# A decoder layer with product-key experts: who makes the low part of the score tiles while the gates are built

## The chip, the cores and the metric

The kernel runs on one core of a Trainium2 chip. The metric is the device time of one execution in microseconds. TensorE (PE) multiplies, VectorE (DVE), ScalarE (ACT) and GpSimd (POOL) compute elementwise, SyncE (SP) issues most of the DMAs. Each engine works through a queue of its own in order, and waits on semaphores for the others.

## What is computed

One hybrid decoder layer over 512 tokens of 1024 features. The first part (a gated DeltaNet mixer beside pooling groups) isn't touched. The second part is the expert mixer:

```python
q = (xb @ w_query).reshape(t, PEER_HEADS, 2, PEER_HALF)
scores = jnp.einsum("thpc,hpkc->thpk", q, sk)
s1, i1 = lax.top_k(scores[:, :, 0], PEER_TOPK)
s2, i2 = lax.top_k(scores[:, :, 1], PEER_TOPK)
...
top_s, top_pos = lax.top_k(cand, PEER_TOPK)
gate = jax.nn.softmax(top_s, axis=-1)
u, v = expert_down[idx], expert_up[idx]
act = jax.nn.gelu(jnp.einsum("td,thkd->thk", xb, u))
return jnp.einsum("thk,thkd->td", (gate * act), v)
```

There are 128 x 128 experts, 8 heads and 16 picks of each head. For 384 of the 512 tokens the kernel works densely: it computes gelu of all 16384 scores, multiplies them by a gate matrix that is zero where nothing was picked, and multiplies the result by expert_up. For the other 128 tokens (NG = 1 block) it gathers the picked rows.

## The kernel before

**Tiles.** The 16384 experts are 128 tiles of 128. A score tile is 8 chunks (c = 0 to 7) of three matmuls each: every float32 operand is split into a high part and a low part, and a chunk is w_hi by xn_hi, w_hi by xn_lo and w_lo by xn_hi (mm3, L126 to L128). A tile's weights come by one DMA of 512 KB into w_raw (L607), ScalarE rounds them to w_hi (L612) and another engine subtracts, w_lo = w_raw - w_hi (L613). w_raw, w_hi and w_lo have two buffers each, so the load of tile n + 2 waits until tile n's low part has been made, and its w_hi until tile n's last matmul with w_hi.

**Stages.** (1) The mixer. (2) Queries and top-16 of the dense tokens, with the first 17 ahead tiles. (3) The gates: the tokens go in 96 groups of four. For a group two sets of one-hot rows are made, oa over the first key and ob over the second, one of them scaled by the gate, and four products g_ps = ob by oa (L857) give the group's gate matrix. In seven groups of ten VectorE makes both (four instructions on L850 and one on L852); in three of ten (A_ACT) it makes ob in one instruction (L841) and ScalarE makes oa in eight (L845, L846). ScalarE copies g_ps into stg (L860); after every eighth group GpSimd copies a part of stg to gsb (L866) and SP writes the rest to memory (gmat, L867). stg has one buffer, oa and ob have four, g_ps has six. (4) The accumulation: per expert tile the gates by the scores, split again, by expert_up into acc (L941), with the scores of the 82 remaining tiles computed, and the 26 stored ones fetched, between, and the gathers of the 128 other tokens on GpSimd and VectorE.

**Ahead tiles in the gates.** 46 score tiles (20 in a run and 26 far ones that go to memory as h_far) are computed ahead of the accumulation, 29 of them by the generator ahead_steps, one chunk at a step. Its steps are taken between the groups (take, 20 before the first group and then 2.2 to a group on average). While tile n runs, at its first step (k = 0), tile n + 1 is loaded and split by load_pair(..., nc.gpsimd). VectorE also works off the picks of the gathered tokens there (pick_gathered, 28 pieces, top-16 by MAX8, FIND_INDEX8 and MATCH_REPLACE8, then L686 to L721), each pinned behind the last one-hot instruction of the group, called one.

**Order.** A scheduler orders each engine's queue; tc.issue_after(x) pins what is traced in its block behind x on x's engine. TensorE's order is pinned throughout this stage by pe_last.

Of the kernel before, what the change touches and what calls it, by code (L numbers as in the profile page):

```python
# [7 lines left out]
F32 = mybir.dt.float32  # L8
# [36 lines left out]
AHEAD = RUN + FAR  # L45
LEAD = 4
FAR_TILES = [RUN + ((2 * k + 1) * (NK - RUN)) // (2 * FAR) for k in range(FAR)]
A_ACT = (1, 4, 7)

C_ID, C_U, C_M0, C_MS, C_IO, C_ONE = 0, 128, 256, 384, 384 + 7 * 128, 384 + 8 * 128  # L50
# [22 lines left out]
def hymba_peer_block(ctx, tc, consts, x, nmix, w_in, w_ba, conv_w, a_log, dt_bias, dn_w, w_pool, pool_scale,  # L73
                     w_out, nffn, w_q, sub_k, downT, down, up, nfin, out):
    nc = tc.nc
# [526 lines left out]

    behind = []

    def load_pair(src, eng):
        raw = wp.tile([P, DC, P], F32, name="w_raw", tag="w_raw")
        nc.sync.dma_start(out=raw, in_=src)  # L607
        hi = wp.tile([P, DC, P], F32R, name="w_hi", tag="w_hi")
        lo = wp.tile([P, DC, P], F32R, name="w_lo", tag="w_lo")
        before = behind.pop(0) if behind else None  # L610
        with tc.issue_after(before) if before is not None else ExitStack():
            nc.scalar.activation(hi, raw, AF.Copy)  # L612
        eng.tensor_sub(lo, raw, hi.bitcast(F32))  # L613
        return hi, lo

    def h_slot(i):
        h_tiles[i] = hp[i % (RUN + 1) >= RA].tile([P, TD], F32, name="h_act")
        return h_tiles[i]


    def s_steps(i, pair):
        hi, lo = pair
        ps = ps_s.tile([P, 512], F32, name="s_ps")[:, :TD]
        for c in range(DC):
            s_last[0] = mm3(ps, (hi[:, c, :], lo[:, c, :]), (xn_hi[:, c, NG * P:], xn_lo[:, c, NG * P:]), c == 0,
                            c == DC - 1)
            if c < DC - 1:
                yield
        if i in FAR_TILES:
            ht = hq.tile([P, TD], F32, name="h_far")  # L630
            s_act[0] = nc.scalar.activation(ht, ps, AF.Gelu)
            nc.sync.dma_start(out=hfar[FAR_TILES.index(i)], in_=ht)
        else:
            s_act[0] = nc.scalar.activation(h_slot(i), ps, AF.Gelu)
        yield
# [3 lines left out]
    def s_tile(i, eng):  # L639
        for _ in s_steps(i, load_pair(downT[i], eng)):  # L640
            pass


    ahead = list(range(RUN)) + FAR_TILES
    made = [0]
# [4 lines left out]
            made[0] += 1  # L650


    def ahead_steps():
        pair = load_pair(downT[ahead[made[0]]], nc.gpsimd)
        while made[0] < AHEAD:
            i, now = ahead[made[0]], pair
            made[0] += 1
            for k, _ in enumerate(s_steps(i, now)):
                if not k and made[0] < AHEAD:
                    pair = load_pair(downT[ahead[made[0]]], nc.gpsimd)  # L660
                yield


    def refill(i):
        if i in FAR_TILES:
            nc.sync.dma_start(out=h_slot(i), in_=hfar[FAR_TILES.index(i)])
        else:
            s_tile(i, nc.vector)
# [55 lines left out]
    def softmax(pool, dst, sc, behind=None):  # L724
        n = sc.shape[1]
        nc.vector.tensor_sub(dst, sc, sc[:, :, 0:1].broadcast_to([P, n, K]))
        with tc.issue_after(behind.ins) if behind is not None else ExitStack():
            nc.scalar.activation(dst, dst, AF.Exp)
        sm = pool.tile([P, n], F32, name="sm", bufs=1)
        nc.vector.tensor_reduce(sm, dst, axis=AX.X, op=ALU.add)  # L730
        nc.vector.reciprocal(sm, sm)
        nc.vector.tensor_tensor(dst, dst, sm[:, :, None].broadcast_to([P, n, K]), op=ALU.mult)

    with ExitStack() as fy:
# [45 lines left out]


        steps = ahead_steps()
        taken = 0
        pe_last = s_last[0]

        def take(goal):
            nonlocal taken, pe_last
            while taken < goal:
                with tc.issue_after(pe_last.ins):
                    next(steps, None)  # L790
                pe_last = s_last[0]
                taken += 1
# [15 lines left out]
    with ExitStack() as fy:  # L808
        hq = fy.enter_context(tc.tile_pool(name="hq", bufs=2))
        t0p = fy.enter_context(tc.tile_pool(name="t0p", bufs=1))  # L810


        def pick_gathered():
            for b in range(NG):
                ts0 = t0p.tile([P, PH, K], F32, name="ts0")
                i10 = t0p.tile([P, PH, K], F32, name="i10")
                i20 = t0p.tile([P, PH, K], F32, name="i20")
                for h in range(0, PH, 2):
                    yield from topk(t0p, sc0[:, b, h:h + 2], 2, ts0[:, h:h + 2], i10[:, h:h + 2], i20[:, h:h + 2])
                softmax(t0p, gat[b], ts0)  # L820
                nc.vector.scalar_tensor_tensor(eidx[b], i10.rearrange("p h k -> p (h k)"), 128.0,
                                               i20.rearrange("p h k -> p (h k)"), op0=ALU.mult, op1=ALU.add)

        picks, picked = pick_gathered(), 0
        n_picks = NG * PH // 2 * 7
        gs = fy.enter_context(tc.tile_pool(name="gs", bufs=3))
        p_g = fy.enter_context(tc.tile_pool(name="p_g", bufs=6, space=PSUM))
        gsb0 = gp.tile([P, NTG, GN * TG], F32, name="gsb")
        n_steps = (AHEAD - S_QUERY - S_WAIT) * DC
        take(S_FIRST)  # L830
        ng = 0
        for tg in range(NTG):
            stg = gs.tile([P, NK, TG], F32, name="stg", bufs=1)
            for q in range(TG // 4):
                oa = gs.tile([P, 4, P], F32, name="oa", bufs=4)
                ob = gs.tile([P, 4, P], F32, name="ob", bufs=4)
                ps = p_g.tile([P, 512], F32, name="g_ps")
                t0 = tg * TG + q * 4
                q4 = [P, 4, P]
                if ng % 10 in A_ACT:  # L840
                    one = nc.vector.tensor_tensor(ob, iota[:, None, :].broadcast_to(q4),  # L841
                                            i2t[:, t0:t0 + 4, None].broadcast_to(q4), op=ALU.is_equal)
                    for u in range(4):
                        t = t0 + u
                        nc.scalar.activation(oa[:, u], iota, AF.Abs, bias=n1t[:, t:t + 1])  # L845
                        nc.scalar.activation(oa[:, u], oa[:, u], AF.Relu, scale=ngt[:, t:t + 1], bias=gtt[:, t:t + 1])  # L846
                else:
                    for u in range(4):
                        t = t0 + u
                        nc.vector.tensor_scalar(ob[:, u], iota, i2t[:, t:t + 1], gtt[:, t:t + 1], op0=ALU.is_equal,  # L850
                                                op1=ALU.mult)
                    one = nc.vector.tensor_tensor(oa, iota[:, None, :].broadcast_to(q4),  # L852
                                            i1t[:, t0:t0 + 4, None].broadcast_to(q4), op=ALU.is_equal)
                ng += 1
                with tc.issue_after(pe_last.ins):
                    for u in range(4):
                        pe_last = nc.tensor.matmul(ps[:, u * P:(u + 1) * P], ob[:, u], oa[:, u], start=(u == 0),  # L857
                                                   stop=(u == 3))
                take(S_FIRST + ng * (n_steps - S_FIRST) // (TD // 4))
                nc.scalar.copy(stg[:, :, q * 4:q * 4 + 4], ps.rearrange("p (t i) -> p i t", i=NK))  # L860
                if ng * n_picks // (TD // 4) > picked:
                    with tc.issue_after(one.ins):
                        next(picks)
                    picked += 1
            sv = stg.rearrange("p i t -> p (i t)")
            nc.gpsimd.tensor_copy(gsb0[:, tg, :], sv[:, :GN * TG])  # L866
            nc.sync.dma_start(out=gmat[tg, :, GN * TG:], in_=sv[:, GN * TG:])  # L867

        for _ in picks:
            pass  # L870

    with ExitStack() as fz:
# [73 lines left out]
        for i in range(NK):  # L946
# [3 lines left out]
            raw = up_p.tile([P, D], F32, name="u_raw", bufs=3)  # L950
# [97 lines left out]
```

## Time and profile before

| | |
|---|---|
| median of three runs | 1597.91 us (1595.98 to 1601.22) |
| the profiled execution | 1597.25 us |
| its span, first to last instruction | 1595.5 us |
| TensorE matmul busy | 1543.3 us, 97% |
| VectorE busy | 1291.3 us, 81% |
| ScalarE busy | 692.1 us, 43% |
| GpSimd busy | 556.9 us, 35% |
| GpSimd's w_lo on L613 | 60 instructions, 153.8 us |
| mean granted TensorE clock | 0.994 |

Busy shares are averages over stages with different limits, so the stage of the gates (483 to 711 us) is to be read by itself. Busy time includes time in which an instruction has begun and doesn't get on. Instructions on VectorE overlap by some 0.08 us where they follow each other, so the cost of one is best read from start to start.

### The profile page before, as it was taken

The page shows a single profiled execution, that of the slowest core. Times are in us where ns is not written, and L with a number is a line of the kernel's source. Part 1 is how long each engine was busy: PE and PEld are TensorE (multiplying, and loading weights), DVE is VectorE, ACT ScalarE, POOL GpSimd, SP SyncE. Part 2 cuts the span into 40 slices and gives each one's busy share as a digit, 9 for nine tenths or more (in the row PEclk, how much of TensorE's full clock was granted, in tenths as well). Part 3 has the DMA queues.
Part 4 walks back from the last instruction along what each step waited for, and adds up shares of the span by engine and source line. Part 5 has one row for each costly group of instructions (what it writes and reads, how often), then busy time and mean ns, then how long its engine had stood idle before and what let it go on. Part 6 is the DMA issues. An engine that isn't in the chain of part 4 may idle for free.

```text
span 1595.5 us, 23368 instructions
## 1 busy us (share of the span) xinstructions
PE 1543.3 (97%) x8417; PEld 1391.5 (87%) x8417; DVE 1291.3 (81%) x2652; ACT 692.1 (43%) x1175; POOL 556.9 (35%) x362
## 2 busy tenths in 40 slices
PE   6999999999999899899999999999999999999996
PEld 5889798888899899889888888889989888888885
DVE  5577666699999999996887777778888787888885
ACT  5545343333338687673333333333333333333333
POOL 1000000144464333224454445444444444444331
PEclk9999999999999999999999999999999999999998
DMA  6221221422344455459999999999999999899971
GB/s 210 80 67 55 65 83 41 172 89 85 93 128 149 175 194 220 153 207 387 364 337 327 339 315 317 329 329 334 311 332 311 335 319 334 309 326 340 321 265 61
DMA packets 142388, 367.32 MB, mean 230 GB/s; under 512 B 11232, under 2 KB 65520, under 8 KB 140608
## 3 DMA queue, kind: packets, MB, share of 16 engines
q1 hardware_dynamic: 104416, 228.09, 41.4%
q0 software_dynamic: 37712, 136.69, 23.9%
q8 instruction: 66, 1.08, 0.3%
q10 hardware_dynamic: 144, 1.05, 0.2%
q14 instruction: 50, 0.41, 0.1%
HBM read 331.58 MB, written 34.21 MB: 229 GB/s over the span
## 4 chain that ended last, share of the span: by engine, by line
PE 80%; DVE 17%; ACT 1%; DMA 1%; issue 1%; POOL 1%; SPq 0%; ACTq 0%; DVEq 0%; POOLq 0%
PE acc L941 33%; PE s_ps L126 9%; PE s_ps L128 9%; PE s_ps L127 9%; DVE ob L850 7%; PE pj L127 3%; PE pj L126 3%; PE pj L128 3%; DVE oa L852 3%; PE q_ps L127 2%; PE q_ps L128 2%; PE q_ps L126 2%; PE ups L432 1%; PE p L441 1%; DVE ob L841 1%; PE sc_ps L762 1%
## 5 line engine op out<-in xcount | busy, mean ns | idle before, releaser
L126 PE MATMUL s_ps<-xn_hi,w_hi 128*128 128x384 f32 x1024 | 356.8, 348 | 0.0
L128 PE MATMUL s_ps<-xn_hi,w_lo 128*128 128x384 f32 x1024 | 346.4, 338 | 2.5 <-DVE w_lo L613 1.9
L127 PE MATMUL s_ps<-xn_lo,w_hi 128*128 128x384 f32 x1024 | 345.7, 338 | 0.0
L612 ACT ACTIVATE w_hi<-w_raw 128x1024 fp32r<-128x1024 f32 x144 | 152.9, 1062 | 331.7 <-PE s_ps L127 260.4
L916 POOL DMA_INDIRECT row<-in_down_dram,eidx x128 | 190.0, 1485 | 224.8 <-DVE row L918 194.4
L925 POOL DMA_INDIRECT row<-in_up_dram,eidx x128 | 187.0, 1461 | 222.8 <-DVE xr L927 201.0
L613 POOL TENSOR_TENSOR w_lo<-w_raw,w_hi 128x1024 fp32r<-128x1024 f32 x60 | 153.8, 2564 | 291.1 <-ACT w_hi L612 257.2
L941 PE MATMUL acc<-u_hi,whi 128*128 128x512 f32 x768 | 238.6, 391 | 0.6 <-ACT whi L120 0.6
L941 PE MATMUL acc<-u_lo,whi 128*128 128x512 f32 x768 | 237.6, 389 | 0.0
L941 PE MATMUL acc<-u_hi,wlo 128*128 128x512 f32 x768 | 237.5, 389 | 0.0
L120 ACT ACTIVATE whi<-w 128x384 fp32r<-128x384 f32 x128 | 67.2, 525 | 307.5 <-issue 277.2
L128 PEld LDWEIGHTS s_ps<-xn_hi,w_lo 128*128 128x128 f32 x1024 | 192.9, 188 | 3.5 <-DVE w_lo L613 2.3
L127 PEld LDWEIGHTS s_ps<-xn_lo,w_hi 128*128 128x128 f32 x1024 | 193.2, 189 | 3.2
L126 PEld LDWEIGHTS s_ps<-xn_hi,w_hi 128*128 128x128 f32 x1024 | 193.2, 189 | 3.2
L121 DVE TENSOR_TENSOR wlo<-w,whi 128x384 fp32r<-128x384 f32 x128 | 71.2, 556 | 133.8 <-ACT whi L120 133.6
L927 DVE SCALAR_TENSOR_TENSOR xr<-row,dots,xr 128x1024 f32<-128x1024 f32 x128 | 164.2, 1282 | 9.6 <-DMA row<-in_up_dram,eidx 7.7
L941 PEld LDWEIGHTS acc<-u_lo,whi 128*128 128x128 f32 x768 | 144.3, 188 | 31.3 <-DVE u_lo L121 0.3
L941 PEld LDWEIGHTS acc<-u_hi,wlo 128*128 128x128 f32 x768 | 144.2, 188 | 29.9
L918 DVE SCALAR_TENSOR_TENSOR row<-row,xg 128x1024 f32<-128x1024 f32 x128 | 152.1, 1220 | 15.0 <-DMA row<-in_down_dram,eidx 11.4
L941 PEld LDWEIGHTS acc<-u_hi,whi 128*128 128x128 f32 x768 | 143.0, 188 | 24.4 <-ACT whi L120 0.8
L121 DVE TENSOR_TENSOR u_lo<-u_raw,u_hi 128x1024 fp32r<-128x1024 f32 x128 | 156.0, 1219 | 4.1 <-ACT u_hi L120 4.1
L120 ACT ACTIVATE u_hi<-u_raw 128x1024 fp32r<-128x1024 f32 x128 | 134.3, 1049 | 5.5 <-DMA u_raw<-in_up_dram 2.8
(298 smaller groups left out, 2448.8 us busy)
## 6 DMA issues: line engine op xcount, KB each, us to landing
u_raw<-in_up_dram SPq DMA_DIRECT2D x128, 512.0 KB, 6.2
w_raw<-in_downT_dram SPq DMA_DIRECT2D x128, 512.0 KB, 5.7
gmat<-stg SPq DMA_DIRECT2D x12, 1984.0 KB, 8.4
gsb<-gmat SPq DMA_DIRECT2D x31, 768.0 KB, 7.3
w_raw<-in_w_in_dram SPq DMA_DIRECT2D x20, 512.0 KB, 3.6
w_raw<-in_w_q_dram SPq DMA_DIRECT2D x16, 512.0 KB, 3.6
hfar<-h_far SPq DMA_DIRECT2D x26, 192.0 KB, 2.0
h_act<-hfar SPq DMA_DIRECT2D x26, 192.0 KB, 5.9
```

What stands on the lines that cost most here:

```text
L120: nc.scalar.activation(hi, src, AF.Copy)
L121: nc.vector.tensor_sub(lo, src, hi.bitcast(F32))
L126: nc.tensor.matmul(ps, ahi, bhi, start=first, stop=False)
L127: nc.tensor.matmul(ps, ahi, blo, start=False, stop=False)
L128: return nc.tensor.matmul(ps, alo, bhi, start=False, stop=last)
L612: nc.scalar.activation(hi, raw, AF.Copy)
L613: eng.tensor_sub(lo, raw, hi.bitcast(F32))
L916: nc.gpsimd.indirect_dma_start(out=r, out_offset=None, in_=down, in_offset=bass.IndirectOffsetOnAxis(ap=eidx[b][:, s:s + 1], axis=0))
L918: nc.vector.scalar_tensor_tensor(r, r, 1.0, xg, op0=ALU.mult, op1=ALU.mult, accum_out=dots[:, s:s + 1])
L925: nc.gpsimd.indirect_dma_start(out=r, out_offset=None, in_=up, in_offset=bass.IndirectOffsetOnAxis(ap=eidx[b][:, s:s + 1], axis=0))
L927: nc.vector.scalar_tensor_tensor(xr[b], r, dots[:, s:s + 1], xr[b], op0=ALU.mult, op1=ALU.add)
L941: nc.tensor.matmul(acc[b][n], l[:, bs], r[:, n * 512:(n + 1) * 512], start=(i == 0 and l is whi and r is uhi), stop=(i == NK - 1 and l is ...
```

## The change

The split is taken apart. load_hi starts the DMA and ScalarE's w_hi as before, at the first step of the tile before. The subtraction is traced later, at that tile's fifth step (k = LO_STEP = 4), goes to VectorE, and is pinned behind dve_one, the one of the newest group. The generator's first load uses VectorE as well. make_ahead and the queries keep GpSimd; in the gates GpSimd is left with its 12 copies.

```diff
+LO_STEP = 4
...
-    def load_pair(src, eng):
+    dve_one = [None]
+
+    def load_hi(src):
         raw = wp.tile([P, DC, P], F32, name="w_raw", tag="w_raw")
         nc.sync.dma_start(out=raw, in_=src)
...
             nc.scalar.activation(hi, raw, AF.Copy)
+        return raw, hi, lo
+
+    def load_pair(src, eng):
+        raw, hi, lo = load_hi(src)
         eng.tensor_sub(lo, raw, hi.bitcast(F32))
         return hi, lo
...
     def ahead_steps():
-        pair = load_pair(downT[ahead[made[0]]], nc.gpsimd)
+        pair = load_pair(downT[ahead[made[0]]], nc.vector)
...
                 if not k and made[0] < AHEAD:
-                    pair = load_pair(downT[ahead[made[0]]], nc.gpsimd)
+                    raw, hi, lo = load_hi(downT[ahead[made[0]]])
+                    pair = (hi, lo)
+                if k == LO_STEP and made[0] < AHEAD:
+                    with tc.issue_after(dve_one[0]) if dve_one[0] is not None else ExitStack():
+                        nc.vector.tensor_sub(lo, raw, hi.bitcast(F32))
                 yield
...
                 ng += 1
+                dve_one[0] = one.ins
```

VectorE's queue at the groups 7 to 10 (counted from 0), before: group 7 is one of ScalarE's (ob alone, L841), 8, 9 and 10 are VectorE's own, and MAX and MAX_INDEX are a piece of the picks.

```order
L841 TENSOR_TENSOR ob<-cst,i2t 128x512
L675 MAX val<-rep 128x8
L676 MAX_INDEX idx<-val,rep 128x8
L850 TENSOR_SCALAR ob<-cst,i2t,gtt 128x128 x4
L852 TENSOR_TENSOR oa<-cst,i1t 128x512
L850 TENSOR_SCALAR ob<-cst,i2t,gtt 128x128 x4
L852 TENSOR_TENSOR oa<-cst,i1t 128x512
L850 TENSOR_SCALAR ob<-cst,i2t,gtt 128x128 x4
L852 TENSOR_TENSOR oa<-cst,i1t 128x512
```

The same place of VectorE's queue in the changed kernel, from group 8 on; its lines are 12 or 13 further on, and L672 is the moved subtraction, here that of tile 22.

```order
L862 TENSOR_SCALAR ob<-cst,i2t,gtt 128x128
L687 MAX val<-rep 128x8
L862 TENSOR_SCALAR ob<-cst,i2t,gtt 128x128
L688 MAX_INDEX idx<-val,rep 128x8
L862 TENSOR_SCALAR ob<-cst,i2t,gtt 128x128 x2
L864 TENSOR_TENSOR oa<-cst,i1t 128x512
L862 TENSOR_SCALAR ob<-cst,i2t,gtt 128x128 x4
L864 TENSOR_TENSOR oa<-cst,i1t 128x512
L672 TENSOR_TENSOR w_lo<-w_raw,w_hi 128x1024
L862 TENSOR_SCALAR ob<-cst,i2t,gtt 128x128 x4
L864 TENSOR_TENSOR oa<-cst,i1t 128x512
```

The subtraction of tile 22 now stands between the rows of the tenth and the eleventh group; in TensorE's queue tile 22's chunks begin after the tenth group's products. The picks are interleaved with the rows one by one.

GpSimd's queue from the mixer's last multiplications into the gates, before (the alternation of subtractions and copies goes on to the twelfth copy).

```order
L477 TENSOR_TENSOR tts<-tt,nfp 128x512 x3
L613 TENSOR_TENSOR w_lo<-w_raw,w_hi 128x1024 x37
L866 COPY gsb<-stg 128x128
L613 TENSOR_TENSOR w_lo<-w_raw,w_hi 128x1024 x2
L866 COPY gsb<-stg 128x128
L613 TENSOR_TENSOR w_lo<-w_raw,w_hi 128x1024 x2
L866 COPY gsb<-stg 128x128
```

GpSimd's queue from the same place in the changed kernel, on to the gathers.

```order
L478 TENSOR_TENSOR tts<-tt,nfp 128x512 x3
L620 TENSOR_TENSOR w_lo<-w_raw,w_hi 128x1024 x31
L879 COPY gsb<-stg 128x128 x12
L929 DMA row<-in_down_dram,eidx_2703 128x1024 x128
L938 DMA row<-in_up_dram,eidx_2703 128x1024 x128
```

29 of GpSimd's 60 subtractions are gone, and its 12 copies follow each other. On SP's queue the write of stg stands behind the load of the same tile as before in ten of the twelve places (the first behind that of tile 24), and one load earlier in the other two; each load waits for the low part of the tile two before it. At the end of the stage TensorE's queue has 28 score matmuls ahead of the first accumulation, and had 12.

## Rows read from the trace of the kernel before

**Rows 1.** The page, chain that ended last: shares of the span by line

```profile
PE acc L941 33%; PE s_ps L126 9%; PE s_ps L128 9%; PE s_ps L127 9%; DVE ob L850 7%; PE pj L127 3%; PE pj L126 3%; PE pj L128 3%; DVE oa L852 3%; PE q_ps L127 2%; PE q_ps L128 2%; PE q_ps L126 2%; PE ups L432 1%; PE p L441 1%; DVE ob L841 1%; PE sc_ps L762 1%
```

**Rows 2.** Windows, last stage: length, busy PE, PEld, DVE, ACT, POOL, clock, DMA

```profile
711.30:1540.00 828.70, 826.84 (x4073) 741.37 (x4074) 666.38 (x831) 295.63 (x404) 377.08 (x256) 1.00 0.93 329
```

**Rows 3.** The same view, four stretches of the gates

```profile
483.10:547.50 64.40, 58.28 (x399) 56.49 (x397) 63.78 (x163) 50.86 (x115) 25.43 (x12) 1.00 0.50 179
547.50:600.90 53.40, 51.45 (x351) 50.87 (x351) 52.71 (x156) 39.73 (x92) 15.99 (x9) 0.97 0.47 164
600.90:657.80 56.90, 48.84 (x339) 47.02 (x337) 56.42 (x151) 40.88 (x95) 19.80 (x10) 1.00 0.60 227
657.80:703.60 45.80, 45.14 (x306) 44.65 (x306) 45.59 (x133) 33.05 (x77) 14.19 (x7) 0.96 0.53 186
```

**Rows 4.** Timeline at long VectorE instructions: start, length, engine, line, what

```profile
494.35 2.88 POOL L613 TENSOR_TENSOR w_lo<-w_raw,w_hi 128x1024 fp32r<-128x1024 f32 x1 [3.00 <-ACT w_hi L612]
...
494.90 3.18 DVE L850 TENSOR_SCALAR ob<-cst,i2t,gtt 128x128 f32<-128x128 f32 x4
...
647.27 2.39 DVE L704 TENSOR_SCALAR ta<-pos 128x32 uint32<-128x32 uint32 x1
...
652.29 2.87 DVE L717 TENSOR_TENSOR oh<-oh,idf 128x1024 bf16<-128x1024 bf16 x1
```

**Rows 5.** VectorE's groups, 483.1 to 711.3: busy us, mean ns | idle before

```profile
L850 DVE TENSOR_SCALAR ob<-cst,i2t,gtt 128x128 f32<-128x128 f32 x268 | 117.4, 489 | 0.0
...
L704 DVE TENSOR_SCALAR ta<-pos 128x32 uint32<-128x32 uint32 x4 | 2.9, 726 | 0.0
```

**Rows 6.** Tiles ob, oa, idf, oh: ns min/median/max, first and last start

```profile
L850 DVE TENSOR_SCALAR ob<-cst,i2t,gtt x268: 320/336/2433, 483.7 to 705.0; 128x128 f32<-128x128 f32 x134
...
L852 DVE TENSOR_TENSOR oa<-cst,i1t x67: 662/679/691, 483.1 to 705.3; 128x512 f32<-128x512 f32 x67
...
L686 DVE CAST idf<-idx x4: 184/313/2399, 523.8 to 690.9; 128x64 bf16<-128x64 uint32 x4
...
L717 DVE TENSOR_TENSOR oh<-oh,idf x4: 685/690/2870, 543.3 to 708.6; 128x1024 bf16<-128x1024 bf16 x4
```

**Rows 7.** L850 by groups in the four stretches, in their order

```profile
L850 DVE TENSOR_SCALAR ob<-cst,i2t,gtt 128x128 f32<-128x128 f32 x73 | 37.1, 564 | 0.0
...
L850 DVE TENSOR_SCALAR ob<-cst,i2t,gtt 128x128 f32<-128x128 f32 x69 | 27.3, 449 | 0.0
...
L850 DVE TENSOR_SCALAR ob<-cst,i2t,gtt 128x128 f32<-128x128 f32 x65 | 28.0, 477 | 0.0
...
L850 DVE TENSOR_SCALAR ob<-cst,i2t,gtt 128x128 f32<-128x128 f32 x60 | 24.9, 459 | 0.0
```

**Rows 8.** GpSimd's groups, 483.1 to 711.3

```profile
L613 POOL TENSOR_TENSOR w_lo<-w_raw,w_hi 128x1024 fp32r<-128x1024 f32 x27 | 70.3, 2605 | 131.6 <-ACT w_hi L612 124.7 <-PE g_ps L857 6.9
L866 POOL COPY gsb<-stg 128x128 f32<-128x128 f32 x12 | 5.7, 473 | 21.7 <-ACT stg L860 21.7
```

**Rows 9.** Timeline, a subtraction on VectorE and the instruction behind it

```profile
711.30 1.22 DVE L613 TENSOR_TENSOR w_lo<-w_raw,w_hi 128x1024 fp32r<-128x1024 f32 x1
712.44 1.02 DVE L958 TENSOR_TENSOR w<-h_act,gsb 128x384 f32<-128x384 f32 x2
```

**Rows 10.** Chain in order of time: last rows of the 10th and 78th group

```profile
506.63 0.60 DVE oa L852
...
664.51 0.60 DVE ob L841
```

**Rows 11.** GpSimd's timeline: the low parts of tiles 22 and 41

```profile
501.71 2.38 POOL L613 TENSOR_TENSOR w_lo<-w_raw,w_hi 128x1024 fp32r<-128x1024 f32 x1 [4.48 <-ACT w_hi L612]
...
666.03 2.96 POOL L613 TENSOR_TENSOR w_lo<-w_raw,w_hi 128x1024 fp32r<-128x1024 f32 x1 [10.71 <-ACT w_hi L612]
```

**Rows 12.** Waits, 483.1 to 711.3: us in total, times, longest

```profile
SPq L607 <- POOL w_lo L613: 65.3, 23, 5.5
...
ACT stg L860 <- DMA gmat<-stg: 9.5, 6, 2.5
```

## Prediction

> **What bounds the kernel now.** I read the chain of waits first, then busy time by stretches, then VectorE's groups and the timeline around its longest instructions. The chain lies on TensorE for most of the span, but 11% of it stands on three lines of one-hot rows, L850, L852 and L841, all VectorE [rows 1]. They belong to one stage, 483.1 to 711.3 us: the gates, 96 groups of one-hot rows and products, with the ahead tiles' score chunks between them. Behind it TensorE is the bound: 826.84 of 828.70 us busy [rows 2]. So whatever the gates stage gives or loses goes through to the end unless the start of the last stage changes.
>
> I cut the stage where TensorE had just waited for rows. VectorE is busy 98.8, 98.7, 99.2 and 99.5% of the four stretches; TensorE sits idle 6.1, 2.0, 8.1 and 0.7 us in them [rows 3]. VectorE sets the first and the third; in the second and fourth both engines are nearly full. The last 8 us of the stage hold no subtraction.
>
> VectorE's 99% isn't all work. While GpSimd makes a low part, four instructions on L850 take 3.18 us; a shift (L704) and a product (L717) met the same way took 2.39 and 2.87 [rows 4]. Over the stage L850 averages 489 ns [rows 5] where its median is 336 [rows 6].
>
> **The change part by part.** *GpSimd's subtractions go* (29, of which 27 in this stage). VectorE's stalls behind them: L850, 268 x (489 - 336) = 41.0 us [rows 5, 6]. L704's four take 2.90 in all, the long one 2.39 [rows 4, 5], so the others 0.17: 2.2 us. L717 2870 - 690 = 2.2; L686 2399 - 313 = 2.1 [rows 6]. Together 47.5. By stretch L850 gives 73 x 228 = 16.6, 69 x 113 = 7.8, 65 x 141 = 9.2 and 60 x 123 = 7.4 us [rows 7]; the long L704 and L717 lie in the third, the long L686 (the last of its four, at 690.9) in the fourth: 16.6, 7.8, 13.6, 9.5. I put all of it down to the subtractions: the 12 copies are a fifth as long [rows 8], and stay. If the stalls that touch a copy and no subtraction stay, it is under 1 us.
>
> *VectorE makes them instead.* From one subtraction's start to the next instruction's start is 712.44 - 711.30 = 1.14 us [rows 9]. The stretches hold 9, 6, 7 and 5 of them (GpSimd's counts of 12, 9, 10 and 7 [rows 3] less three, three, three and two copies): 10.3, 6.8, 8.0, 5.7 us, 30.8 in all. VectorE's work so changes by -6.3, -1.0, -5.6 and -3.8, which is -16.7 us.
>
> *What of it reaches the end.* TensorE can't go below its own work, so a stretch gains at most its idle time: min(6.3, 6.1) + min(1.0, 2.0) + min(5.6, 8.1) + min(3.8, 0.7) = 6.1 + 1.0 + 5.6 + 0.7 = 13.4 us.
>
> *The first two unpinned subtractions* (tiles 17 and 18) stand where VectorE waits for transposes and for the exponential; I take 0, at most 2 x 1.14. Tile 19's stands ahead of the first one-hot row and is among the 27.
>
> *The new wait.* A subtraction on VectorE waits for ScalarE's w_hi, with the next group's rows and picks queued behind it, and TensorE waits for those. The order puts tile 22's behind the tenth group's rows. In the trace those rows end at 506.63 + 0.60 = 507.23, and its w_hi had been there at 501.7, when GpSimd began: 5.5 us of slack. The tightest I found is tile 41, behind the 78th group: rows done at 665.11, w_hi at 666.0, a wait of 0.9 [rows 10, 11]. That is a stretch where VectorE was well ahead of TensorE, so the wait takes from a lead. I take 0; the bound is 27 x 0.9 = 24 us.
>
> *The deadline.* TensorE needs the low part for the third matmul of the tile. The order puts the subtraction just after the rows of the last group ahead of the tile, so 1.14 us runs beside that group's eight products and two matmuls. I take 0; in three tiles (24, 26, 37) it stands one group later, where TensorE may wait some 1.4 us but finds the next rows ready: 0 to 4.
>
> *The queues.* SP's load into the freed w_raw slot now waits for a subtraction that comes some 5 us later, and behind four of these loads (before the copies of groups 8, 16, 80 and 88) stands the write of stg, whose slot ScalarE's next copy waits for. SP already waited 65.3 us for low parts, ScalarE 9.5 for that write, 2.5 at most [rows 12]. ScalarE's own rows for three groups in ten are queued behind such a copy. Bounds: 0, and 4 x 2.5 = 10; I take 2, since ScalarE has lead there.
>
> *Start of the last stage.* 16 score matmuls move ahead of the first accumulation, under the wait for the first weights: 0 to -0.6 us; I take 0.
>
> Sum: -13.4 + 2 = -11.4. The profiled execution took 1597.25 us (span 1595.5 and 1.75 around it), 0.66 below the median of the runs shown: 1597.25 - 11.4 = 1585.9, so 1586.
>
> **A rule against it.** L852 has two SBUF inputs, like the subtraction, and its 67 executions stay between 662 and 691 ns although GpSimd subtracts for 70 us of the stage [rows 6, 8]; the product L717, with two inputs as well, was held once. The Trainium skill (SBUF — State Buffer, Who interferes with whom) says that a VectorE instruction with two SBUF inputs contends with a GpSimd instruction that reads SBUF; by that rule, which the L852 row doesn't bear out, the moved subtractions could still wait for the copies, at most 12 x 0.47 = 5.7 us, an estimate, and the sum would be 1591.6.
>
> **The rivals.** *VectorE's whole saving comes through* (TensorE's idle time was only where I cut): 16.7 us, and the granted clock, on average 0.97 and 0.96 of the 2.4 GHz level in the second and fourth stretch [rows 3], comes back whole, 0.03 x 53.4 + 0.04 x 45.8 = 3.4 us: 1577 to 1581. Against it: TensorE is full in the fourth stretch.
>
> *Lead is capped, queues cost more.* Where VectorE is ahead it now waits for w_hi and can't store the lead that the picks' heavy ends use up; with the queues' 5 us half the gain goes: 1590 to 1593.
>
> *The in-order wait takes the gain's place.* If ScalarE's w_hi comes late because ScalarE stands before a stg write, each subtraction holds VectorE. The point: 16.7 / 27 = 0.6 us each cancels the saving. At 0.4 to 0.7 the time is within 0.3%. At 1.0 it is 27 - 16.7 = 10 us slower, 1607. For it: tile 41's 0.9; against: 5.5 us of slack at tile 22, and a wait that comes only with a lead.
>
> *It doesn't do what it says*: the pin only bounds the place from above, and the order shows the subtraction far behind the pinned row, at the tile's edge rather than in mid-tile. That changes the deadline, not VectorE's work, so it has no time and no chance of its own.
>
> **How the numbers follow.** Forecast, 1581 to 1590: 0.55. Whole saving: 0.10. Capped: 0.13. Cancelled, within 0.3%: 0.15. Slower: 0.07. What a measurement of this kernel can tell is about 0.3%, 4.8 us, so faster is below 1593.1: 0.78; same 0.15; slower 0.07. The range 1580 to 1596 leaves out half of the whole saving and the upper part of the last two cases, under 0.2 together.
>
> **What the changed profile would show.** L850's mean falls from 489 to some 340 ns with no instruction over 1 us; VectorE has 27 more subtractions of 1.22 us in the stage; the stage shrinks from 228 to some 216 us, and the rest keeps its length. Wrong would be: VectorE idle before its subtractions, released by ScalarE's w_hi, by more than 5 us; TensorE idle on ScalarE's rows by more than the before; or L850 still stretched.

## The result, and the profile of the changed kernel

The changed kernel took 1575.1 us (median of four runs) against 1597.35 for the kernel before on the same chip: a ratio of 0.9849, 95% interval 0.9837 to 0.9862. That is 22 us faster, twice the 11.4 forecast and 5 us below the low end of the range. The direction was right, the size was not. The profiled execution took 1572.2 us (span 1570.4); it started the changed stage 3.7 us earlier than the profiled execution of before, 2.8 of that in work that neither kernel changes. The first score matmul of the runs below lies anywhere from 323.0 to 327.0 us, whatever the kernel. So I compare lengths inside the trace, and medians.

The page of the changed kernel, chain that ended last, by engine and by line (11% on one-hot rows in [rows 1]):

```profile
PE 92%; DVE 3%; ACT 2%; DMA 2%; issue 1%; POOL 0%; SPq 0%; ACTq 0%; DVEq 0%; POOLq 0%
...
PE acc L954 33%; PE s_ps L127 11%; PE s_ps L129 11%; PE s_ps L128 11%; PE g_ps L870 4%; PE pj L128 3%; PE pj L127 3%; PE pj L129 3%; PE q_ps L128 2%; PE q_ps L127 2%; PE q_ps L129 2%; PE ups L433 1%; PE p L442 1%; DMA gmat<-stg 1%; PE sc_ps
```

No row of VectorE's one-hot lines is left among the named ones. Its groups in the gates stage, 479.5 to 690 us (busy us, mean ns | idle before), where [rows 5] had L850 at 489 ns:

```profile
L862 DVE TENSOR_SCALAR ob<-cst,i2t,gtt 128x128 f32<-128x128 f32 x268 | 78.5, 336 | 0.0
L864 DVE TENSOR_TENSOR oa<-cst,i1t 128x512 f32<-128x512 f32 x67 | 45.6, 681 | 0.0
L672 DVE TENSOR_TENSOR w_lo<-w_raw,w_hi 128x1024 fp32r<-128x1024 f32 x27 | 32.8, 1215 | 0.0
```

The mean is the old median, and the tile's row shows no long instruction (min/median/max; 2433 at most in [rows 6]):

```profile
L862 DVE TENSOR_SCALAR ob<-cst,i2t,gtt x268: 317/336/451, 480.6 to 679.8; 128x128 f32<-128x128 f32 x134
```

VectorE waits for nothing before its 27 subtractions. The windows of the changed kernel, cut at the same instructions as [rows 3] (the first products of groups 25, 49 and 72) and at the last product, and then the last stage (length, busy PE, PEld, DVE, ACT, POOL, clock, DMA share; compare [rows 2, 3]):

```profile
479.50:536.30 56.80, 56.80 (x398) 56.80 (x397) 56.56 (x175) 48.28 (x110) 1.24 (x3) 1.00 0.48 173
536.30:587.00 50.70, 49.86 (x354) 49.28 (x352) 50.35 (x158) 40.67 (x94) 0.89 (x3) 1.00 0.57 204
587.00:636.70 49.70, 48.16 (x338) 47.60 (x339) 49.46 (x160) 39.95 (x93) 3.07 (x3) 1.00 0.59 223
636.70:686.60 49.90, 49.09 (x345) 48.27 (x344) 49.54 (x159) 40.87 (x92) 0.66 (x3) 1.00 0.59 210
691.30:1500.00 808.70, 808.70 (x3983) 724.54 (x3982) 651.03 (x814) 287.20 (x393) 373.05 (x253) 1.00 0.93 330
```

TensorE and VectorE are both busy for nearly all of the stage now, and the granted clock is at the 2.4 GHz level in all four stretches (it was 0.97 and 0.96 of it in two of [rows 3]).

**Where the time went**, from the starts of the same instructions in the traces (us; the last two runs are explained below):

| stretch | before | changed | e6 | e7 |
|---|---|---|---|---|
| first: products of groups 0 to 25 | 58.84 | 51.28 | 58.89 | 51.28 |
| second: groups 25 to 49 | 53.38 | 50.61 | 51.95 | 52.32 |
| third: groups 49 to 72 | 56.90 | 49.71 | 57.18 | 48.75 |
| fourth: group 72 to the end of the last product | 50.83 | 49.88 | 50.98 | 52.19 |
| last product to first accumulation | 4.90 | 4.77 | 4.78 | 4.88 |
| score matmuls in that gap | 12 | 28 | 28 | 12 |
| first to last accumulation | 868.79 | 866.05 | 866.04 | 868.80 |

The gates stage gives 18.5 us, the start of the last stage 0.1 + 2.7, and the stretch from the first score matmul to the transposes before the gates 0.9: 22.2.

**VectorE's own account.** I added up, for every VectorE instruction from the first one-hot row with the gate (L850, L862) to the end of the last pick (eidx), the time from its start to the start of the next one. In both kernels there is no gap over 60 ns in it, so this sum is the length of the stretch:

| us, start to start | before | changed | difference |
|---|---|---|---|
| one-hot rows with the gate (L850, L862) | 109.53 | 68.18 | -41.35 |
| cast, shifts and product of the picks (tiles idf, ta, oh) | 11.04 | 4.14 | -6.90 |
| subtractions (26 of the 27 lie in the stretch) | 0 | 29.49 | +29.49 |
| everything else | 106.70 | 103.40 | -3.30 |
| the whole stretch | 227.27 | 205.21 | -22.06 |

VectorE's stretch is 22.06 us shorter, and the time fell by 22.2, of which 0.9 lies ahead of the stage. One row block of oa (0.60 us) stands ahead of this stretch in the kernel before and inside it in the changed one; with the same rows counted, "everything else" fell by 3.9.

### The profile page after: what moved, and what is told of

It is laid out like the page before. It is cut to its first block, busy times and chain, and to the rows that moved or that the text cites. A ratio compares the mean times of both kernels' runs of the same rounds, so it can differ in the third digit from the quotient of the medians.

```text
span 1570.4 us, 23360 instructions
## 1 busy us (share of the span) xinstructions
PE 1535.9 (98%) x8417; PEld 1387.4 (88%) x8417; DVE 1272.1 (81%) x2681; ACT 692.2 (44%) x1175; POOL 481.7 (31%) x333
## 4 chain that ended last, share of the span: by engine, by line
PE 92%; DVE 3%; ACT 2%; DMA 2%; issue 1%; POOL 0%; SPq 0%; ACTq 0%; DVEq 0%; POOLq 0%
PE acc L954 33%; PE s_ps L127 11%; PE s_ps L129 11%; PE s_ps L128 11%; PE g_ps L870 4%; PE pj L128 3%; PE pj L127 3%; PE pj L129 3%; PE q_ps L128 2%; PE q_ps L127 2%; PE q_ps L129 2%; PE ups L433 1%; PE p L442 1%; DMA gmat<-stg 1%; PE sc_ps L774 1%
## 5 line engine op out<-in xcount | busy, mean ns | idle before, releaser
L931 DVE SCALAR_TENSOR_TENSOR row<-row,xg 128x1024 f32<-128x1024 f32 x128 | 151.9, 1219 | 16.8 <-DMA row<-in_down_dram,eidx 16.7
L620 POOL TENSOR_TENSOR w_lo<-w_raw,w_hi 128x1024 fp32r<-128x1024 f32 x31 | 77.1, 2488 | 154.8 <-ACT w_hi L615 128.0
```

The lines of the kernel that those rows point to most:

```text
L931: nc.vector.scalar_tensor_tensor(r, r, 1.0, xg, op0=ALU.mult, op1=ALU.mult, accum_out=dots[:, s:s + 1])
```

## Experiments

Ratios are to the kernel before on the same chip.

**e3: no low parts in the stage.** The third matmul of each chunk reads the high part again, so the kernel leaves out that correction to the scores.

```diff
-                    raw, hi, lo = load_hi(downT[ahead[made[0]]])
-                    pair = (hi, lo)
-                if k == LO_STEP and made[0] < AHEAD:
-                    with tc.issue_after(dve_one[0]) ...:
-                        nc.vector.tensor_sub(lo, raw, hi.bitcast(F32))
+                    raw, hi, lo = load_hi(downT[ahead[made[0]]], low=False)
+                    pair = (hi, hi)
```

> The changed kernel without the low parts of tiles 18 to 45: nobody subtracts, the third matmul of each of their chunks reads the high part again. Left out: that correction to the scores. VectorE loses 27 x 1.14 = 30.8 us of work in the gates stage, and nothing comes back on GpSimd. Theory TensorE (VectorE now runs ahead and TensorE's own work sets the stage): the stage can shrink only from 201.5 us towards TensorE's packed floor of some 196, so 1570 to 1573 us against 1575.1, and VectorE shows some 25 us of idle time in the stage, waiting for free row buffers. Theory VectorE (VectorE's 99% busy share says that it still sets the stage): 15 us or more come off, 1560 or less. By the prediction's step (a stretch gains at most TensorE's idle time, now 3.2 us): 1572 to 1575.

Measured: 1568.2 us, ratio 0.9815 (0.980 to 0.983). Its window from the end of the transposes to the last product, and its gate rows:

```profile
482.70:684.50 201.80, 201.80 (x1430) 201.75 (x1430) 182.77 (x623) 168.83 (x387) 7.09 (x11) 1.00 0.57 207
```

```profile
L859 DVE TENSOR_SCALAR ob<-cst,i2t,gtt 128x128 f32<-128x128 f32 x268 | 76.8, 340 | 14.3 <-PE g_ps L867 14.0
```

Here TensorE has no gap at all, and VectorE waits for it (16.7 us of gaps). This is TensorE's floor: taking away 29.5 us of VectorE's work gives only 5 to 7 us more. The theory that TensorE's work is close holds; it is reached some 5 us below the changed kernel.

**e4: a third of the subtractions made twice on VectorE.**

```diff
                         nc.vector.tensor_sub(lo, raw, hi.bitcast(F32))
+                        if made[0] % 3 == 0:
+                            nc.vector.tensor_sub(lo, raw, hi.bitcast(F32))
```

> The changed kernel with every third moved subtraction made twice on VectorE: 9 more of 1.13 us in the gates stage, 10.2 us of VectorE's work, nothing else. Theory VectorE (it has no gap between its rows from the first row to the last pick, so every us of its work is a us of the time, both ways, until TensorE's floor some 5 us below): 1575.1 + 10.2 = 1585. Theory TensorE (it is 98.5% busy in the stage and VectorE a median 3.1 us ahead of it, so TensorE sets the stage now and VectorE has something in hand): 1575 to 1578.

Measured: 1582.57 us, ratio 0.9897 (0.9882 to 0.9912), 7.5 us more than the changed kernel's 1575.1. VectorE's stretch is 212.89 us, 7.7 more: the nine repeated subtractions cost the 10.2 expected, and the searches of the picks were 1.6 us shorter, because rows now stand behind all of them (see the account of VectorE's term below). So VectorE has nothing in hand in the changed kernel, although the chain names TensorE: what its stretch grows by comes out whole, what it shrinks by only down to e3's floor.

**e5 and e8: GpSimd gets something to do again**, in a scratch tile that nobody reads; VectorE keeps its subtractions. The order on every other engine is the changed kernel's, instruction for instruction.

```diff
                         nc.vector.tensor_sub(lo, raw, hi.bitcast(F32))
+                    nc.gpsimd.tensor_sub(scr, raw, hi.bitcast(F32))     # e5
+                    nc.gpsimd.tensor_copy(scr, raw)                     # e8
```

> The changed kernel with the same 27 subtractions made a second time on GpSimd, into a scratch tile that nobody reads; VectorE's own stay, in the same order. It prices GpSimd's instruction for VectorE. Theory contention: each one stretches VectorE's rows by some 47.5 / 27 = 1.76 us; the rows' mean on the one-hot line goes back from 336 to about 490 ns, and the time from 1575 to 1575 + 47.5 less the few us that TensorE has in hand, 1615 to 1625. Rival (the long rows of before came from the wait for low parts and its queues, not from GpSimd's instruction itself): rows stay at 336 ns and the time within 5 us of 1575.

> The changed kernel with one plain copy of w_raw (128x1024, one input) per tile on GpSimd into a scratch tile that nobody reads, at the places where the run with GpSimd's second subtractions had those. Theory any (whatever GpSimd does with SBUF holds VectorE's one-input rows): rows' mean well above 336 ns, the time up by tens of us, towards that run's 1630. Theory two inputs (only GpSimd's two-input subtraction does): rows' mean 336 to 345 ns, time 1574 to 1579.

Measured: e5 1630.0 us, ratio 1.0203 (1.0182 to 1.0223); e8 1592.15 us, ratio 0.9961 (0.9945 to 0.9976). The groups of GpSimd and VectorE in the stage, e5 first:

```profile
L674 POOL TENSOR_TENSOR scr<-w_raw,w_hi 128x1024 fp32r<-128x1024 f32 x28 | 77.4, 2766 | 157.7 <-ACT w_hi L616 122.6 <-issue 33.8 <-POOL gsb L881 1.3
...
L864 DVE TENSOR_SCALAR ob<-cst,i2t,gtt 128x128 f32<-128x128 f32 x268 | 117.6, 481 | 0.0
...
L673 DVE TENSOR_TENSOR w_lo<-w_raw,w_hi 128x1024 fp32r<-128x1024 f32 x28 | 39.2, 1399 | 0.7 <-ACT w_hi L616 0.7
```

```profile
L674 POOL COPY scr<-w_raw 128x1024 f32<-128x1024 f32 x27 | 40.1, 1485 | 148.7 <-DMA w_raw<-in_downT_dram 148.7
...
L864 DVE TENSOR_SCALAR ob<-cst,i2t,gtt 128x128 f32<-128x128 f32 x268 | 94.5, 396 | 0.0
```

The long rows come back with GpSimd's instruction alone, though nobody waits for its result. VectorE's stretch grows by 53.4 us in e5 (258.59), 2.0 for each subtraction of 2.77, and the time by 55; the rival that blamed the wait for low parts falls. The plain copy holds VectorE too, 16.9 us or 0.63 for each copy of 1.49, so the theory that only a two-input GpSimd instruction does falls as well: e8 lies between its two expectations.

**e6 and e7: the subtractions of two of the four stretches on VectorE**, the others on GpSimd where before had them.

```diff
+                    if not on_vector(made[0]):
+                        nc.gpsimd.tensor_sub(lo, raw, hi.bitcast(F32))
-                if k == LO_STEP and made[0] < AHEAD:
+                if k == LO_STEP and made[0] < AHEAD and on_vector(made[0]):
+    on_vector = 28 <= n <= 33 or n >= 41        # e6: second and fourth
+    on_vector = n <= 27 or 34 <= n <= 40        # e7: first and third
```

> Only the low parts of tiles 28 to 33 and 41 to 45 (second and fourth stretch of the gates stage) on VectorE, those of the first and third on GpSimd as before. Theory of the prediction (a stretch gains at most its TensorE idle time): 1.0 + 0.7 = 1.7 us, so 1595.7. Theory carry (VectorE's saving comes through whole, wherever it falls, and the start of the last stage gains where VectorE is ahead at the stage's end): 1.0 + 3.8 = 4.8 and up to 2.7 at the start of the last stage, so 1590 to 1593.

> Only the low parts of tiles 17 to 27 and 34 to 40 (first and third stretch) on VectorE, those of the second and fourth on GpSimd as before. Theory of the prediction: 6.1 + 5.6 = 11.7 us, 1585.7, with groups 24 to 48 keeping their 56.2 us. Theory carry: 6.3 + 5.6 = 11.9 and the slow matmuls that went with the stalls, some 2 us, so 1582 to 1586; VectorE enters the second stretch ahead, so groups 24 to 48 shorten by 2 us or more although their own low parts are GpSimd's; the start of the last stage gains nothing.

Measured: e6 1592.57 us, ratio 0.9968 (0.9956 to 0.9979); e7 1579.99 us, ratio 0.9903 (0.9885 to 0.9920). The medians are 5.3 and 17.9 us below before, 23.1 together: the two halves add up to about the whole change. The prediction's cap allowed 1.7 and 11.7. The table of stretches shows how e7 breaks it, with 15.4 us in the stage: the first stretch gains 7.56 where TensorE had 6.1 us idle, the third 8.15 where VectorE's saving was put at 5.6, and the second shortens by 1.1 us although six of its low parts are still GpSimd's and one subtraction more lies on VectorE there. VectorE's rows are 1.72 us ahead of the product at its start (0.15 in the kernel before). That carry is half of what I expected for groups 24 to 48. Part of the third's gain is work that crossed the cut: some 3.5 us of a pick's last pieces stand in the third stretch before and in the fourth in e7, and e7's fourth is 1.4 us longer. Together the two gain 6.8 us, still more than the cap's 5.6. e6 speaks against the carry theory inside the stage (1.0 us gained there, where that theory had 4.8 and the cap 1.7), and gets 2.8 us more at the start of the last stage; of the rest of its 5.3, 0.9 lies ahead of the stage.

**e1: no pin.**

```diff
-                    raw, hi, lo = load_hi(downT[ahead[made[0]]])
-                    pair = (hi, lo)
-                if k == LO_STEP and made[0] < AHEAD:
-                    with tc.issue_after(dve_one[0]) ...:
-                        nc.vector.tensor_sub(lo, raw, hi.bitcast(F32))
+                    pair = load_pair(downT[ahead[made[0]]], nc.vector)
```

> The subtractions on VectorE as in the changed kernel, but written where the kernel before writes them (right behind w_hi, with no pin). The order of instructions on each engine comes out the same as the changed kernel's, row for row. Theory engine (only the engine matters, the pin and the place in the program change nothing): 1575 and the stage 201.5 us from its first product to its last. Rival (the pin does something that the order doesn't show): more than 5 us away from that.

Measured: 1575.2 us, ratio 0.9844 (0.9826 to 0.9863), 202.0 us from the first product to the last. The order of instructions on every engine is the changed kernel's. The pin and the place in the program do nothing here; the change is the engine.

**e9: 32 groups instead of 29 with one row block from ScalarE**, twice.

```diff
-                if ng % 10 in A_ACT:
+                if ng % 3 == 1:
```

> The changed kernel with 32 instead of 29 of the 96 groups having one of their two row blocks made by ScalarE (every third group): VectorE loses 3 x 4 x 0.254 = 3.1 us of work, ScalarE gets 3 x 4 x (0.494 + 0.403) = 10.8 us, on top of some 192 of 207 us. Theory VectorE: up to 3.1 us faster, 1572. Rival ScalarE (at 97% it becomes late with rows and with the evictions that free the product tiles): 1577 to 1585.

> The kernel with 32 groups' rows partly on ScalarE again, beside the one without the pin on the same chip. If VectorE's work still sets the stage, it is 2 to 3 us faster than that (1572 against 1575, stage 199 against 201.5 us); if TensorE or ScalarE does, no difference that can be told.

Measured: 1571.6 us, ratio 0.9831 (0.9818 to 0.9845), and 1573.63 us, ratio 0.9838 (0.9822 to 0.9854). In the traces the products take 198.95 and 198.80 us against 201.49 and 202.0 without it, so the stage is 2.5 and 3.2 us shorter, near the 3.1 us of work that VectorE lost (its stretch is 1.9 and 2.5 us shorter). It is faster than the kernel before, but its intervals overlap the changed kernel's: the gain over that is seen in the stage, not yet in the time. ScalarE was busy for 169.8 of 207.1 us in the changed kernel, less than the 192 that I had started from. In this run it pays in waits for the write of stg (waits, us in total, times, longest):

```profile
ACT stg L873 <- DMA gmat<-stg: 11.6, 8, 3.1
```

**e11: the kernel before, with two-input gate rows.**

```diff
-                    for u in range(4):
-                        nc.vector.tensor_scalar(ob[:, u], iota, i2t[..], gtt[..], op0=ALU.is_equal, op1=ALU.mult)
+                    nc.vector.tensor_tensor(ob, iota.., i2t.., op=ALU.is_equal)
+                    nc.vector.tensor_tensor(ob, ob, gtt.., op=ALU.mult)
```

> The kernel before, with GpSimd's subtractions where they were, and only the form of the one-hot rows with the gate changed: instead of four one-input instructions of 128x128 per group (L850, 4 x 109.53 / 268 = 1.63 us from start to start with their stalls) VectorE issues two two-input instructions of 128x512 (compare, then multiply by the gate; about 0.60 us each from start to start, as L852). Same result. Theory form (GpSimd holds the one-input rows and hardly ever a two-input instruction): VectorE's work in the stage falls by 109.5 - 67 x 1.2 = 29 us, below TensorE's, and the time comes to TensorE's floor, 1569 to 1573. Rival (any VectorE instruction with SBUF inputs is held, two inputs above all): the 27 stalls of 1.5 to 1.9 us stay, VectorE's saving is no more than some 67 x (1.02 - 1.2) = -12 us, and the time is 1597 or above.

Measured: 1608.79 us, ratio 1.0061 (1.0042 to 1.008): slower than before. My theory fell outright. The tiles ob and oa (min/median/max), and the timeline around one of GpSimd's subtractions, GpSimd first:

```profile
L848 DVE TENSOR_TENSOR ob<-cst,i2t x67: 666/680/2881, 479.4 to 716.3; 128x512 f32<-128x512 f32 x67
L850 DVE TENSOR_TENSOR ob<-ob,gtt x67: 667/681/2868, 482.8 to 717.5; 128x512 f32<-128x512 f32 x67
...
L851 DVE TENSOR_TENSOR oa<-cst,i1t x67: 665/680/2898, 480.0 to 716.9; 128x512 f32<-128x512 f32 x67
```

```profile
515.27 2.76 POOL L613 TENSOR_TENSOR w_lo<-w_raw,w_hi 128x1024 fp32r<-128x1024 f32 x1 [5.69 <-ACT w_hi L612]
```

```profile
515.70 2.88 DVE L851 TENSOR_TENSOR oa<-cst,i1t 128x512 f32<-128x512 f32 x1
518.51 0.68 DVE L850 TENSOR_TENSOR ob<-ob,gtt 128x512 f32<-128x512 f32 x1
```

The row that starts 0.43 us after GpSimd's subtraction ends 0.55 us after it. There are 26 VectorE instructions over 1.5 us in the stage, about one for each of the 27 subtractions, most of them two-input rows. The hold doesn't depend on this form: it falls on the row that happens to stand there.

## Why the prediction was wrong, step by step

**What bounds the kernel: right, and more than was said.** VectorE sets the stage from the first row to the last pick. Across the kernels the time follows the length of that stretch of VectorE:

| kernel | stretch | time | time less stretch |
|---|---|---|---|
| e9 | 203.3 | 1571.6 | 1368.3 |
| changed | 205.2 | 1575.1 | 1369.9 |
| e1 | 206.0 | 1575.2 | 1369.2 |
| e7 | 211.3 | 1580.0 | 1368.7 |
| e4 | 212.9 | 1582.6 | 1369.7 |
| e8 | 222.2 | 1592.2 | 1370.0 |
| e6 | 223.0 | 1592.6 | 1369.6 |
| before | 227.3 | 1597.4 | 1370.1 |
| e5 | 258.6 | 1630.0 | 1371.4 |

(Times are medians, the stretches those of the profiled executions. e3 is left out because VectorE has gaps there. e11, counted from its first multiplication by the gate, has 240.4 us and 1368.4.)

**GpSimd's subtractions go: right.** 47.5 us of stalls were forecast; by start to start the same groups lost 41.35 + 6.90 = 48.25. (A reading beside it was off without consequence: VectorE's share of the first stretch is 99.0% by [rows 3], not 98.8.)

**VectorE makes them instead: right, but the order was left out.** 30.8 forecast for 27, 29.5 measured for the 26 in the stretch, 1.13 each. Not foreseen: the rest of VectorE's work was 3.3 us shorter (3.9 with the same rows counted), 3.6 of it in the searches of the picks. Where a search has the next step of its own pick behind it, it takes longer from start to start than where a row has come between. The first two lines are from the kernel before, the last two from the changed one, where the next instruction starts 0.32 and 0.21 us after the search:

```profile
508.78 0.28 DVE L671 MAX8 val<-sc 128x8 f32<-128x128 f32 x1
509.10 0.09 DVE L672 MATCH_VALUE_LOAD idx<-val,sc 128x8 f32 x1
...
501.14 0.28 DVE L683 MAX8 val<-sc 128x8 f32<-128x128 f32 x1
501.35 0.67 DVE L853 TENSOR_TENSOR ob<-cst,i2t 128x512 f32<-128x512 f32 x1
```

In all twelve traces MAX8 and MATCH_REPLACE8 take 176 to 213 ns with a row or a subtraction behind them and 288 to 330 with the pick's next step. Of the 72 in the stretch, 42 had that step behind them in the kernel before and in e3, 13 in the changed kernel, e1, e5 and e8, and none in e4. The 29 that changed give 29 x 0.12 = 3.4 us. So this part of the gain came from the new order of VectorE's queue and not from GpSimd. The prediction had no term for it, though the order shown with the change has it. VectorE's change is -22.06 instead of -16.7: 0.75 and 1.3 from the two terms, 3.3 from this.

**What of it reaches the end: the step that failed.** "TensorE can't go below its own work, so a stretch gains at most its idle time", and the sum of four minima, 13.4. The stage gave 18.5 by the products' starts, more than the minimum in every stretch:

| stretch | minimum forecast | measured | VectorE's rows shorter by | their lead at its start, before and changed |
|---|---|---|---|---|
| first | 6.1 | 7.56 | 8.17 | 1.86, 2.81 |
| second | 1.0 | 2.77 | 1.21 | 0.15, 1.70 |
| third | 5.6 | 7.19 | 7.91 | 0.15, 0.15 |
| fourth | 0.7 | 0.95 | 3.34 | 0.15, 0.87 |

(The fourth column compares the time from the rows of the first group of a stretch to those of the next one's; the last is the time from a group's rows to its first product.) Two things were wrong in the cap. First, TensorE's busy time is not its own work. From the first product to the last all kernels run the same matmuls (in e3 a third of the score matmuls read another operand); these are the windows of the kernel before, the changed kernel and e3:

```profile
488.75:708.70 219.95, 203.16 (x1397) 198.44 (x1397) 217.75 (x605) 163.95 (x375) 72.09 (x37) 0.98 0.52 187
485.08:686.57 201.49, 198.30 (x1397) 196.34 (x1397) 200.30 (x637) 164.28 (x375) 5.86 (x11) 1.00 0.56 204
488.32:684.45 196.13, 196.13 (x1397) 196.08 (x1397) 177.15 (x606) 163.21 (x375) 7.09 (x11) 1.00 0.58 210
```

TensorE is busy for 203.16, 198.30 and 196.13 us with them. So 4.9 us of what I had taken as work went with the waits, and 7.0 of it is gone where nothing makes TensorE wait. The granted clock, 0.97 of the 2.4 GHz level in the second and in the fourth of these stretches before and 1.00 after, is a part of it. It is not all: in the first stretch, with 1.00 in both kernels, busy time fell from 52.63 to 51.28 as well. That is how the first stretch could gain 7.56: it stands at 51.28 us in the changed kernel, e7 and e3 alike, which is TensorE's floor there.

Second, the cuts. What VectorE gained beyond that floor was not lost: in the second stretch its 1.21 and the 1.55 of lead brought in make the 2.77. In the fourth, of its 3.34 and the 0.72 of lead brought in 0.95 came out, and the rest left the stage as lead: the last group's rows are 4.79 us ahead of their products, and were 1.68. The third is another error, of VectorE's term: the order places the subtractions later than GpSimd had run them, so the stretches held 7, 7, 6 and 6 (as counted between the rows) rather than 9, 6, 7 and 5, and the third had room for VectorE's larger saving. Of the 5.1 us missed in the stage, the 1.6 of the third stretch are VectorE's term and 1.6 of the second the lead; the 1.5 of the first took both, since the cap stood at 6.1 and VectorE's saving at 6.3.

The rival that named this, "VectorE's whole saving comes through", had the mechanism and 1577 to 1581; I gave it 0.10 because TensorE looked full in the fourth stretch. It missed too: it had VectorE's saving 5.4 us too small, and the 3.4 us that it added for the clock show up as no term beside VectorE's stretch in the table above.

**Start of the last stage: mis-sized.** It was taken as 0 with -0.6 at most, and is -2.7. The gap before the first accumulation keeps its length with 16 more score matmuls in it, 16 x 0.175 = 2.8 us. Before, the 12 matmuls filled 2.1 of 4.90 us; the other 2.8 were idle and free for the taking, and [rows 2] already showed 1.86 of them. e7 keeps the order of before there, and its chain shows the same steps on VectorE that the kernel before has:

```profile
693.53 0.20 DVE eidx L838
...
694.09 1.22 DVE w_lo L623
695.31 0.48 DVE w L976
...
695.81 0.53 ACT whi L121
...
696.38 0.73 PE acc L959 x2
```

In the changed kernel VectorE has passed eidx 0.8 us before the last product ends (before: 2.25 us after it), and the chain stays on TensorE up to the accumulation:

```profile
685.68 0.89 PE g_ps L870 x8
686.57 0.17 PE s_ps L127
686.75 0.17 PE s_ps L128
```

**The new wait and the deadline: right at 0.** VectorE idles 0.0 us before L672. TensorE's waits in the stage are for rows alone (3.1 us, 2.3 of them for ScalarE's, which were 2.9 before), none for a low part.

**The queues: 2 us taken, none seen.** ScalarE's wait for the write of stg fell from 9.5 us [rows 12] to 6.4, and the time less VectorE's stretch is no longer than before's:

```profile
ACT stg L873 <- DMA gmat<-stg: 6.4, 4, 2.8
```

**Unpinned subtractions: 0 taken.** The stretch that holds them, from the first score matmul to VectorE's copy of the last transposes, is 0.9 us shorter in the changed kernel, within what it varies by between the other runs (156.4 to 157.7 us).

**The rule against it.** The prediction set a row against the Trainium skill (SBUF — State Buffer, Who interferes with whom), by which a two-input VectorE instruction contends with a GpSimd instruction that reads SBUF. e11 shows that the rule holds here: two-input rows of up to 2.90 us. The inference from L852's 662 to 691 ns was wrong, and the trace of before already had the answer:

```profile
488.35 3.00 POOL L613 TENSOR_TENSOR w_lo<-w_raw,w_hi 128x1024 fp32r<-128x1024 f32 x1 [2.32 <-ACT w_hi L612]
...
488.44 0.68 DVE L852 TENSOR_TENSOR oa<-cst,i1t 128x512 f32<-128x512 f32 x1
...
489.04 3.18 DVE L850 TENSOR_SCALAR ob<-cst,i2t,gtt 128x128 f32<-128x128 f32 x4
```

The row kept its 0.68 us, the subtraction beside it took 3.00, and the gate row behind the row was held. Five L852 rows start within 0.11 us of a subtraction's start; the subtractions there take 2.89 to 3.05 us, where the shortest of the stage takes 2.36. So it was GpSimd that waited for these rows, for some 0.6 us each. What decides which of the two goes first, no run here shows. In the changed kernel the same is seen once more: VectorE's subtractions stay at 1201 to 1226 ns, and one of the 12 copies that remain, otherwise 0.30 to 0.48 us long, takes 2.46 beside two two-input rows and a subtraction:

```profile
619.84 2.46 POOL L879 COPY gsb<-stg 128x128 f32<-128x128 f32 x1 [16.34 <-ACT stg L873]
```

So the estimate of 5.7 us had the right pair of engines and the wrong one waiting, and it cost the sum nothing.

## What to carry to other kernels

When one engine runs without a gap through a stage, forecast the stage from that engine's sum of start-to-start times, and bound it below by the other engine's spacing where nothing makes it wait, not by its busy time less idle time in each piece. Work that was moved to an idle GpSimd beside a VectorE that sets the time is not free: price it by the VectorE instruction it holds, and compare with what VectorE needs to do it itself. If a row looks immune to a hold, look whether the other engine's instruction beside it has grown instead. And read a new order for more than the moved instruction: here it also put rows between searches that had stood back to back, and 3.4 us came from that.

## What the runs showed of the hardware

A GpSimd subtraction of 128x1024 that takes 2.4 to 3.1 us holds one VectorE instruction until it ends, 1.8 us of VectorE's time on average in the kernel before (48.25 / 27) and 2.0 in e5; VectorE does the same subtraction in 1.13. A copy of the same tile on GpSimd, 1.49 us, costs VectorE 0.63 on average. Held were one-input rows with two scalars, casts, shifts and, in e11, two-input compares and products alike; the searches (MAX8 and those behind it) and reductions were not seen to be held. The hold goes the other way too: beside a two-input row the subtraction took 3.00 us instead of 2.36, and a small copy 2.46 instead of 0.3. A MAX8 or MATCH_REPLACE8 costs VectorE some 0.12 us more where the pick's next step stands right behind it than where a row does.
